# Where the modulation's last four vectors are computed: beside the delta-net heads, or beside the branch merge

## The chip, the cores and the metric

One Trainium2 chip, one of its cores. The kernel is one program that runs once. The time is device microseconds (us) of that run. The kernel before took 2231.86 us (median of 3 runs, 2228.46 to 2231.94). The engines are named as in the profile: PE (matrix unit; PEld its weight loads), DVE (vector), ACT (scalar), POOL (general), and SP, which here only issues DMAs.

## The reference

One layer of a streaming encoder, on x of 1024 positions by 1024 channels, all in float32. The parts that matter here, shortened:

```python
mod = (silu(c) @ w_ada + b_ada)[:, None, :]            # 1024 -> 6 * 1024
shift_t, scale_t, gate_t, shift_f, scale_f, gate_f = split(mod, 6)
h = x * (1 + scale_t) + shift_t
proj = h @ w_in                                        # split into the inputs of both branches
o_a = gated_deltanet(...)                              # 8 heads, chunked delta rule
o_b = chunk_band_attention(...)                        # 16 heads, 9-chunk band
merged = gate_a * (o_a @ w_branch_a) + gate_b * (o_b @ w_branch_b)
x = layernorm(ALPHA * x + gate_t * (merged @ w_o))
h = x * (1 + scale_f) + shift_f
...                                                    # up-projection, conv, product, down-projection
x = layernorm(ALPHA * x + gate_f * ffn)
```

`shift_t` and `scale_t` are needed at once. The other four vectors of `mod` are needed late: `gate_t` when `w_o` is prepared in the merge, `shift_f` and `scale_f` after the first layer norm, `gate_f` in the down-projection. They are what is moved: 4096 numbers, each a dot product of 1024 terms.

## The kernel before, in words

Large products are made exact by splitting each float32 operand in a high part (a cast by ACT) and a low part (the rest: source minus high part, by DVE or POOL), and adding three matmuls: high by high, high by low, low by high. A weight block of 1024 x 128 is loaded by one DMA of 512 KB into a tile `raw`, cast to `wh` on ACT and subtracted to `wl` on POOL (`wblock`, L275). `raw`, `wh` and `wl` have three buffers each. They are handed out in the order in which the code asks for them: a load into `raw` can be issued only when the tile three requests earlier has been read for the last time. All these loads are on SP's queue, which issues in its own order and stops at the first one that may not start.

The stages are: modulation of x and first projections (to about 90 us); eight delta-net heads, each with a triangular solve, an inverse and a chain over 8 steps, with projections woven between them (to about 870); sixteen attention heads (to about 1347); the merge (L1036 to L1077), which starts while attention still runs; the output projection `mix` with layer norm (from 1459.5); up- and down-projection.

The merge has two branches of eight blocks. Below, a0 to a7 are the blocks of branch A and b0 to b7 those of branch B. A block is 48 matmuls, 24 for each half of the positions, into one PSUM bank (`pbr`). Branch A's banks are 0 and 1: DVE's scaling by the gate (`ma`, L1054) frees a bank. Branch A multiplies `o_a`, which lies in `hh` and `hl`. Branch B multiplies `o_b`, whose eight row blocks are loaded back from `ob_d` through `raw` and split (`load_split`, L1065): ob0 and ob1 are asked for after a5, ob2 to ob4 after a6, ob5 to ob7 after a7. During branch B the rows of `w_o` also pass through `raw`: they are scaled by `gate_t` (L1075) and split.

The four late vectors were made in `mod_rows` (L804), called twice per head. Sixteen halves m0 to m15, two for each 512 columns: a half loads four 128 x 512 pieces of `w_ada` in two DMAs through `raw`, and DVE multiplies each by `silu(c)` and adds it to an accumulator (`gt` ring, 2 slots, shared with the gates' outputs). After an odd half PE sums the accumulator over partitions with a matrix of ones (`pmod`), DVE adds the bias, and the row goes to memory (`mod_d`). After the merge `shift_f` and `scale_f` came back from `mod_d` and were transposed on PE (`pmr`, L1119).

The code is handed to a scheduler that simulates the program and fixes each engine's order in advance. Engines then run in that order and wait for each other by semaphores.

Of the kernel before, what the change touches and what calls it, by code (L numbers as in the profile page):

```python
# [17 lines left out]
P = 128  # L18
# [55 lines left out]
def _at(group, step_, n, first=0):  # L74
    return tuple((group, first + step_ * i) for i in range(n))
# [26 lines left out]
    "bt": _at("GA", 640, 2), "sb": (*_at("GA", 640, 4, 1280), ("FA", 384)),  # L102
    "ot": (("GA", 3840), ("FA", 0)), "mx": _at("FA", 4, 8, 256),

    "gb": _at("GB", 512, 2), "macc": _at("M", 0, 1), 
    "st": _at("ST", 12, 2), "mv": _at("ST", 4, 4, 36), "gtb": (MA[0],), "g1b": (_E1[1],),
    "b1b": (_E1[2],), "r": (_E1[3], ("GL", 0)), "x1": _at("GL", 1024, 2, 1024),
    "h2": _at("GL", 0, 1, 3072),
# [46 lines left out]
def hybrid_layer(  # L155
# [646 lines left out]
    macc = [None]  # L802

    def mod_rows(i):  # L804

        cb = i // 2
        if i % 2 == 0:
            macc[0] = ring("gt", [P, 512])
        acc = macc[0]
        for k0 in range(4 * (i % 2), 4 * (i % 2) + 4, 2):  # L810
            rv = W.tile([P, 2, 512], F32, tag="raw", bufs=RB, name=nm("raw"))
            SP.dma_start(rv, w_ada2[k0 * P:(k0 + 2) * P,
                                    2 * D + 512 * cb:2 * D + 512 * cb + 512].rearrange(
                                        "(k p) n -> p k n", p=P))
            for k in (k0, k0 + 1):
                if k == 0:
                    DVE.tensor_scalar(acc, rv[:, 0, :], csil[:, 0:1], None, ALU.mult)
                else:
                    DVE.scalar_tensor_tensor(acc, rv[:, k - k0, :], csil[:, k:k + 1], acc,
                                             ALU.mult, ALU.add)  # L820
        if i % 2 == 1:
            pr_ = mtile(nm("pmod"), "i")
            PE.matmul(pr_, ones, acc, start=True, stop=True)
            row = ring("gt", [P, 512])[0:1, :]
            SP.dma_start(row, b_ada[:, 2 * D + 512 * cb:2 * D + 512 * cb + 512])
            DVE.tensor_tensor(row, row, pr_[0:1, :], ALU.add)
            SP.dma_start(mod_d[:, 512 * cb:512 * cb + 512], row)
# [13 lines left out]
    for h in range(HA):  # L841
        ORD = "sigKq"
        for o in ORD:
            if o == "s":
                with tc.high_priority(offset=PF):
                    stage_solve(h, cs[h])
            elif o == "i":
                with tc.high_priority(offset=PI):
                    stage_inverse(h, cs[h])
            elif o == "K" and h + 1 < HA:  # L850
                with tc.issue_after(last.ins) if last else nullcontext():
                    cs.append(stage_k(h + 1))
            elif o == "g":
                some_gates(GA[h])
            elif o == "q" and h + 1 < HA:
                stage_q(h + 1, cs[h + 1])
        some_gates(GB[h])
        for i in (2 * h, 2 * h + 1):
            mod_rows(i)
        if h + 1 < HA:  # L860
            stage_vz(h + 1, cs[h + 1])
        with tc.high_priority(offset=PC):
            stage_chain(h, cs[h])
        with tc.high_priority(offset=PT):
            stage_out(h, cs[h])
        last = cs[h]["last"]
# [163 lines left out]
    def bcast(key, src):  # L1030
        t_ = ring(key, [P, D])
        SP.dma_start(t_, src.partition_broadcast(P).rearrange("p o n -> p (o n)"))
        return t_

    wo = []
    for br in range(2):  # L1036
        if br == 1:
            mh, ml = (t_.rearrange("p k s -> p (k s)").rearrange("p (t k q) -> p t k q", t=NT, k=NK)
                      for t_ in (hh, hl))
        rh, rl = ((oahk, oalk), (obh, obl))[br]  # L1040
        for j in range(NK):
            w = wblock(kview(wbr[br], j * P, P), NK)
            for n in range(2):
                N = slice(512 * n, 512 * n + 512)
                ps = pbank(nm("pbr"), "ab"[br])
                for k in range(NK):
                    for a, r in ((w[0], rh), (w[0], rl), (w[1], rh)):
                        PE.matmul(ps, a[:, k, :], r[k][:, N],  # L1048
                                  start=(k == 0 and a is w[0] and r is rh),
                                  stop=(k == NK - 1 and a is w[1]))  # L1050
                gt_ = ma[j][:, N] if br == 0 else ring("gb", [P, 512])
                SP.dma_start(gt_, gates_d[br * NK + j][:, N])
                if br == 0:
                    DVE.scalar_tensor_tensor(gt_, gt_, 1.0, ps, ALU.add, ALU.mult)  # L1054
                else:
                    DVE.scalar_tensor_tensor(gt_, gt_, 1.0, ps, ALU.add, ALU.mult)
                    POOL.tensor_tensor(gt_, gt_, ma[j][:, N], ALU.add)
                    T4 = slice(4 * n, 4 * n + 4)
                    split(mh[:, T4, j, :], ml[:, T4, j, :],
                          gt_.rearrange("p (t q) -> p t q", t=4), ACT, DVE)  # L1060
                    if "merged" in dbg:
                        SP.dma_start(dbg["merged"][j * P:j * P + P, N], gt_)
            if br == 0:
                for k in {5: (0, 1), 6: (2, 3, 4), 7: (5, 6, 7)}.get(j, ()):
                    load_split(obh[k], obl[k], ob_d[k], ACT, DVE)  # L1065
            if br == 1 and j == 0:
                gtb = bcast("gtb", mod_d[:, 0:D])
                DVE.tensor_scalar(gtb, gtb, 0.5, None, ALU.mult)
            if br == 1 and j and (j % 2 == 0 or j == NK - 1):

                for k in ([j // 2 - 1] if j < NK - 1 else range(3, NK)):
                    a, b = (place(o, [P, D], F32R, "wo") for o in (*MA[1:], *OB[:9])[2 * k:2 * k + 2])
                    raw = W.tile([P, D], F32, tag="raw", bufs=RB, name=nm("raw"))
                    SP.dma_start(raw, w_o2[k * P:k * P + P, :])
                    DVE.tensor_tensor(raw, raw, gtb, ALU.mult)  # L1075
                    split(a, b, raw, ACT, DVE)
                    wo.append((a, b))  # L1077
# [508 lines left out]
```

## Time and profile before

| What | us |
|---|---|
| median of 3 runs | 2231.86 |
| the profiled execution: its own time | 2233.05 |
| its span, first to last instruction | 2231.3 |
| attention's last matmul, from where PE only does merge blocks | 1346.15 |
| last merge block ends, `mix` begins | 1459.52 |

The profile is of one execution. A row of a timeline gives the start, the duration, the engine, the line, what is written from what, and in brackets how long the engine stood idle before it and who ended that. Several instructions of a kind are merged in a row with xN. Rows with SPq are DMA issues. Matmuls overlap in the pipeline, so a matmul of 392 ns is followed by the next after about 228 ns. A full-precision product is recorded as two matmuls.

### The profile page before, as it was taken

To read this page: it belongs to the slowest core of one execution; us is meant where nothing else is said; L and a number is where in the kernel's file an instruction comes from. 1 tells how busy PE (TensorE), PEld (TensorE's weight loads), DVE (VectorE), ACT (ScalarE), POOL (GpSimd) and SP (SyncE) were. 2 spreads that over 40 slices of the span, in tenths; PEclk is the share of its full clock that TensorE was granted. 3 is DMA by queue.
4 is the path that set the end of the run, shared out by engine and by line. 5 is a ranking of instruction groups with operands and counts; after the bars stand their busy time and mean duration, and the time that the engine had idled before them with its cause. 6 is when DMAs were issued, how large, how long until landed. Compare 5 with 4: busy or idle time off the path is not lost.

```text
span 2231.3 us, 31605 instructions
## 1 busy us (share of the span) xinstructions
PE 2129.5 (95%) x11469; PEld 1781.7 (80%) x11469; DVE 1575.9 (71%) x3234; ACT 1032.8 (46%) x2196; POOL 607.2 (27%) x554
## 2 busy tenths in 40 slices
PE   6998999999999999999999999999899999999997
PEld 5787787777878787798989788888688888888875
DVE  7467585765667764567776653456998888889998
ACT  4645253434434334467675642234554444455532
POOL 4323232332222322234342423433010000000064
PEclk9999999999999999999999999999999999999999
DMA  9232333423232412211111424342222222243213
GB/s 277 83 110 79 95 92 106 119 74 112 81 98 92 135 36 84 80 53 51 60 63 63 148 95 132 109 137 95 65 96 85 85 85 85 85 189 129 108 48 132
DMA packets 227263, 220.48 MB, mean 99 GB/s; under 512 B 27354, under 2 KB 184467, under 8 KB 227107
## 3 DMA queue, kind: packets, MB, share of 16 engines
q1 hardware_dynamic: 227027, 218.44, 30.9%
q8 instruction: 90, 1.47, 0.3%
q14 instruction: 66, 0.54, 0.1%
q10 hardware_dynamic: 80, 0.03, 0.0%
HBM read 177.48 MB, written 47.23 MB: 101 GB/s over the span
## 4 chain that ended last, share of the span: by engine, by line
PE 45%; DVE 6%; issue 1%; ACT 1%; DMA 0%; POOL 0%; DVEq 0%; SPq 0%; ACTq 0%
PE pup L1296 18%; PE pbr L1048 8%; PE pdn L1470 6%; PE pwo L1110 4%; PE pqk L885 2%; PE pv L900 2%; PE po L975 2%; PE pp L960 1%; PE ps L934 1%; DVE hh L1536 0%; DVE hh L1507 0%; DMA raw<-in_w_branch_a_dram 0%; DVE dop L181 0%; DVE hl L181 0%; DVE hh L1506 0%
## 5 line engine op out<-in xcount | busy, mean ns | idle before, releaser
L181 POOL TENSOR_TENSOR wl<-raw,wh 128x1024 fp32r<-128x1024 f32 x88 | 211.7, 2408 | 325.1 <-ACT wh L178 295.6
L1296 PE MATMUL pup<-hh,wop 128*128 128x512 f32 x704 | 226.8, 392 | 0.4 <-ACT hh L178 0.4
L1296 PE MATMUL pup<-t,wop 128*128 128x512 f32 x792 | 191.3, 395 | 5.5 <-DVE wop L181 3.3
L1296 PEld LDWEIGHTS pup<-t,wop 128*128 128x128 f32 x792 | 149.6, 189 | 39.5 <-DVE wop L181 3.7
L1296 PEld LDWEIGHTS pup<-hh,wop 128*128 128x128 f32 x704 | 133.0, 189 | 29.5 <-ACT hh L178 0.8
L178 ACT CAST wh<-raw 128x1024 fp32r<-128x1024 f32 x88 | 92.4, 1050 | 136.3 <-DMA raw<-in_w_in_dram 57.3
L285 PE MATMUL pqkv<-hh,wh 128*128 128x512 f32 x352 | 143.3, 408 | 0.0
L285 PE MATMUL pqkv<-hl,wh 128*128 128x512 f32 x352 | 141.2, 401 | 0.0
L285 PE MATMUL pqkv<-hh,wl 128*128 128x512 f32 x352 | 140.0, 399 | 0.0
L1296 PE MATMUL pup<-hl,wop 128*128 128x512 f32 x352 | 137.9, 392 | 1.7 <-DVE hl L181 1.7
L664 DVE TENSOR_TENSOR FT<-FT,G 128x16 f32<-128x16 f32 (+30 forms) x248 | 120.7, 487 | 19.5 <-POOL G L609 12.2
L178 ACT CAST wop<-wr 128x512 fp32r<-128x512 f32 x110 | 67.8, 621 | 124.7 <-DVE wr L1282 62.9
L945 POOL TENSOR_SCALAR G<-G,FT 128x640 f32<-128x640 f32 (+4 forms) x103 | 69.9, 681 | 182.9 <-DVE FT L944 161.9
L1337 POOL TENSOR_TENSOR cc<-cc,G 128x512 f32<-128x512 f32 x15 | 26.2, 1751 | 265.7 <-DVE G L1319 222.7
L181 DVE TENSOR_TENSOR wop<-wr,wop 128x512 fp32r<-128x512 f32 x110 | 80.7, 740 | 25.1 <-ACT wop L178 25.0
L285 PE MATMUL pgt<-hh,wl 128*128 128x512 f32 x240 | 95.1, 396 | 0.8 <-POOL wl L181 0.8
L285 PE MATMUL pgt<-hh,wh 128*128 128x512 f32 x240 | 95.4, 397 | 0.1
L285 PE MATMUL pgt<-hl,wh 128*128 128x512 f32 x240 | 94.7, 395 | 0.0
L964 DVE TENSOR_TENSOR pl<-pp,ph 128x512 fp32r<-128x512 f32 (+2 forms) x116 | 72.5, 635 | 17.2 <-ACT ph L963 16.4
L1470 PE MATMUL pdn<-hl 128*128 128x512 f32 x324 | 78.2, 395 | 4.9 <-DVE hh L1484 4.6
L942 ACT ACTIVATE G<-G,FT 128x640 f32<-128x640 f32 (+4 forms) x103 | 71.6, 696 | 18.9 <-DVE FT L937 16.9
L1296 PEld LDWEIGHTS pup<-hl,wop 128*128 128x128 f32 x352 | 66.6, 189 | 16.2 <-DVE hl L181 2.1
(457 smaller groups left out, 6163.2 us busy)
## 6 DMA issues: line engine op xcount, KB each, us to landing
raw<-in_w_in_dram SPq DMA_DIRECT2D x72, 512.0 KB
wr<-in_w_up_dram SPq DMA_DIRECT2D x44, 512.0 KB
raw<-in_w_ada_dram SPq DMA_DIRECT2D x32, 512.0 KB
dr<-g_d SPq DMA_DIRECT2D x18, 512.0 KB
dr<-in_w_down_dram SPq DMA_DIRECT2D x18, 512.0 KB
wa<-in_w_ada_dram SPq DMA_DIRECT2D x32, 256.0 KB
gates_d<-GT SPq DMA_DIRECT2D x32, 256.0 KB
g_d<-yy SPq DMA_DIRECT2D x15, 512.0 KB
```

What stands on the lines that cost most here:

```text
L178: ACT.copy(h, src)
L181: return le.tensor_tensor(l, src, f(h), ALU.subtract).ins
L285: PE.matmul(ps, a[:, k, :], r[k][:, 512 * n:512 * n + 512], start=(k == 0 and a is wh and r is rh), stop=(k == NK - 1 and a is wl))
L664: DVE.tensor_tensor(pr[:, :, 0:i + 1], ft[:, :, 0:i + 1], fa[:, i:i + 1, 0:i + 1].to_broadcast([P, 8, i + 1]), ALU.mult)
L885: PE.matmul(ps, a[:, k, :], r[:, k, 512 * n:512 * n + 512], start=(k == 0 and a is w[0] and r is hh), stop=(k == NK - 1 and a is w[1]))
L942: ACT.activation(sb[:, 0:n], sb[:, 0:n], AF.Exp, bias=mx[:, nb - 1:nb], scale=-1.0, accum_out=mx[:, 2:3])
L945: POOL.tensor_scalar(sb[:, 0:n], sb[:, 0:n], mx[:, 3:4], 0.0, ALU.mult, ALU.add)
L964: DVE.tensor_tensor(pl[:, B, :], pp, f(ph[:, B, :]), ALU.subtract)
L1048: PE.matmul(ps, a[:, k, :], r[k][:, N], start=(k == 0 and a is w[0] and r is rh), stop=(k == NK - 1 and a is w[1]))
L1110: PE.matmul(ps[n], a[:, t, k, :], wo[k][b][:, 512 * n:512 * n + 512], start=(k == 0 and a is mh and b == 0), stop=(k == NK - 1 and a is ml))
L1296: PE.matmul(ps, a[:, u, k, :], b[v][k], start=(new and k == 0 and u == 0 and v == 0), stop=(k == 3 and u == 1), skip_group_check=not new)
L1470: PE.matmul(sets[s_][i], a[:, u, i * P:i * P + P], b[:, v, :], start=(new and j == 0 and u == 0 and v == 0), stop=(j == nq - 1 and u == 1) ...
```

## The change

The halves m0 to m15 leave the delta-net heads. They are now made by `mod_half`, which a table places behind blocks of the merge: m0 and m1 behind a5, m2 and m3 behind a6, m4 behind a7, and eleven halves behind b0 to b6. The accumulator has a ring of two slots of its own (in the space `B4`). For `gate_t` and `gate_f` the row goes to memory as before. For `shift_f` and `scale_f` four small matmuls by one column of ones put the sums straight into columns, and DVE adds the bias from `vt` there, so the load and the transpose after the merge are gone. In the merge, the block of branch weights is asked for two blocks ahead of its use in the code.

```diff
-    "gb": _at("GB", 512, 2), "macc": _at("M", 0, 1), 
+    "gb": _at("GB", 512, 2), "macc": _at("M", 512, 2), 
...
-    def mod_rows(i):
...
-        for i in (2 * h, 2 * h + 1):
-            mod_rows(i)
...
+    def mod_half(i):
+        cb = i // 2
+        if i % 2 == 0:
+            macc[0] = ring("macc", [P, 512])
+        acc = macc[0]
...
+        if i % 2 == 0:
+            return
+        pr_ = pbank(nm("pmod"), "mod")
+        if 2 <= cb < 6:
+            for q in range(4):
+                PE.matmul(pr_[:, q:q + 1], acc[:, q * P:q * P + P], ones[:, 0:1], start=True, stop=True)
+            o, v = 8 + 4 * (cb - 2), VO["b_ada"] + 16 + 4 * cb
+            DVE.tensor_tensor(aff[:, o:o + 4], pr_[:, 0:4], vt[:, v:v + 4], ALU.add)
+        else:
+            PE.matmul(pr_, ones, acc, start=True, stop=True)
+            row = acc[0:1, :]
...
+    MODS = {(0, 5): (0, 1), (0, 6): (2, 3), (0, 7): (4,), (1, 0): (5, 6), (1, 1): (7,), (1, 2): (8, 9), (1, 3): (10,),
+            (1, 4): (11, 12), (1, 5): (13,), (1, 6): (14, 15)}
+    def branch_block(i):
+        return wblock(kview(wbr[i // NK], i % NK * P, P), NK)
+    wnext = [branch_block(i) for i in range(2)]
...
-            w = wblock(kview(wbr[br], j * P, P), NK)
+            w = wnext.pop(0)
+            if NK * br + j + 2 < 2 * NK:
+                wnext.append(branch_block(NK * br + j + 2))
...
+            for i in MODS.get((br, j), ()):
+                mod_half(i)
             if br == 0:
                 for k in {5: (0, 1), 6: (2, 3, 4), 7: (5, 6, 7)}.get(j, ()):
                     load_split(obh[k], obl[k], ob_d[k], ACT, DVE)
...
-    mrow = ring("macc", [P, P])[0:16, :]
-    SP.dma_start(mrow, mod_d[:, D:3 * D].rearrange("o (r p) -> (o r) p", p=P))
-    pmr = pbank("pmr", "t")
-    PE.transpose(pmr[:, 0:16], mrow, ident[0:16, 0:16])
```

What stands where now, at three places. First SP's queue at the end of attention. Before, with `raw_12899` the weights of a7, ob0 to ob2 already ahead of it and `ob_d<-ob_12023` the store of the last attention output:

```order
L186 DMA raw_12899<-in_w_branch_a_dram 128x8x128
L186 DMA raw_12893<-ob_d 128x1024
L186 DMA raw_12961<-ob_d 128x1024
L186 DMA raw_13040<-in_w_branch_b_dram 128x8x128
L1117 DMA B_1594_12402<-mod_d 16x128
L186 DMA raw_12889<-ob_d 128x1024
L1013 DMA ob_d<-ob_12023 128x1024
L1052 DMA FT_12403<-gates_d 128x512 x2
L186 DMA raw_12965<-ob_d 128x1024
L186 DMA raw_12957<-ob_d 128x1024
```

Of the change, from the weights of a7 (`raw_12604`) on, `ob_d<-ob_11855` being the same store:

```order
L186 DMA raw_12604<-in_w_branch_a_dram 128x8x128
L1018 DMA raw_12662<-in_w_ada_dram 128x2x512
L1018 DMA raw_12666<-in_w_ada_dram 128x2x512
L1018 DMA raw_12670<-in_w_ada_dram 128x2x512
L1018 DMA raw_12674<-in_w_ada_dram 128x2x512
L984 DMA ob_d<-ob_11855 128x1024
L1068 DMA FT_12235<-gates_d 128x512 x2
L186 DMA raw_12683<-ob_d 128x1024
L186 DMA raw_12687<-ob_d 128x1024
L186 DMA raw_12693<-in_w_branch_b_dram 128x8x128
L1018 DMA raw_12751<-in_w_ada_dram 128x2x512
```

The loads of m0 and m1 stand ahead of the store now, and all eight loads of `ob_d` behind it; before, six of them stood ahead.

Second, DVE in the change, from the half of a4 that it scales second (`pbr_12575`); L1023 and L1025 are the products of m0 and m1, `ob_11855` is the last attention output that waits for PE, L181 is the split of ob0. Before, none of the L1023 and L1025 stood here:

```order
L1070 SCALAR_TENSOR_TENSOR ma_12241<-ma_12241,pbr_12575 128x512
L1023 TENSOR_SCALAR B_1554_12234<-raw_12662,csil 128x512
L1025 SCALAR_TENSOR_TENSOR B_1554_12234<-raw_12662,csil,B_1554_12234 128x512
L952 TENSOR_TENSOR ob_11855<-po_12217,FT_7141 64x256
L1025 SCALAR_TENSOR_TENSOR B_1554_12234<-raw_12666,csil,B_1554_12234 128x512 x2
L1070 SCALAR_TENSOR_TENSOR ma_12242<-ma_12242,pbr_12608 128x512
L1025 SCALAR_TENSOR_TENSOR B_1554_12234<-raw_12670,csil,B_1554_12234 128x512 x2
L1025 SCALAR_TENSOR_TENSOR B_1554_12234<-raw_12674,csil,B_1554_12234 128x512 x2
L1070 SCALAR_TENSOR_TENSOR ma_12242<-ma_12242,pbr_12635 128x512
```

The scalings that free branch A's banks stand behind products that need a load.

Third, PE in the change, where a6 ends (`pbr_12724`), a7 begins (`pbr_12790`) and the second half of a7 (`pbr_12817`) is cut by `pmod`. Before, each half's 24 matmuls stood together and in the order of the blocks. `pbr_12870` is b0:

```order
L1064 MATMUL pbr_12724<-hh,wl_12543 128x512
L1064 MATMUL pbr_12870<-ob_12245,wh_12691 128x512
L1064 MATMUL pbr_12870<-ob_12251,wh_12691 128x512
L1064 MATMUL pbr_12870<-ob_12245,wl_12692 128x512
L1064 MATMUL pbr_12870<-ob_12246,wh_12691 128x512
L1064 MATMUL pbr_12790<-hh,wh_12602 128x512
```

And a little further on:

```order
L1064 MATMUL pbr_12817<-hh,wh_12602 128x512
L1064 MATMUL pbr_12817<-hl,wh_12602 128x512
L1036 MATMUL pmod_12767<-B_1554_12234,ones 128x512
L1064 MATMUL pbr_12817<-hh,wl_12603 128x512
L1064 MATMUL pbr_12817<-hh,wh_12602 128x512
```

Four matmuls of b0 stand ahead of a7, and PE must have m3 finished to go on in a7. Further on PE's row has b0, its second half and b1 in pieces: 11 of b0's first half, 15 of its second, 4 of b1, then the rest mixed.

More of the change, by code (lines that the diff above doesn't have):

```diff
@@ L800, in gate_block @@
             SP.dma_start(gates_d[j][:, N], gt_)
-    macc = [None]
-    def mod_rows(i):
[L806 to L827, printed above, removed]
     gate_block(0)
@@ L1033, in bcast @@
         return t_
+    aff = cst.tile([P, 24], F32, tag="aff", name="aff")
+    macc = [None]
+    def mod_half(i):
[3 more added lines that the diff above has]
+        acc = macc[0]
+        for k0 in range(4 * (i % 2), 4 * (i % 2) + 4, 2):
+            rv = W.tile([P, 2, 512], F32, tag="raw", bufs=RB, name=nm("raw"))
+            SP.dma_start(rv, w_ada2[k0 * P:(k0 + 2) * P,
+                                    2 * D + 512 * cb:2 * D + 512 * cb + 512].rearrange(
+                                        "(k p) n -> p k n", p=P))
+            for k in (k0, k0 + 1):
+                if k == 0:
+                    DVE.tensor_scalar(acc, rv[:, 0, :], csil[:, 0:1], None, ALU.mult)
+                else:
+                    DVE.scalar_tensor_tensor(acc, rv[:, k - k0, :], csil[:, k:k + 1], acc,
+                                             ALU.mult, ALU.add)
+        if i % 2 == 0:
[6 more added lines that the diff above has]
+            DVE.tensor_tensor(aff[:, o:o + 4], pr_[:, 0:4], vt[:, v:v + 4], ALU.add)
+        else:
+            PE.matmul(pr_, ones, acc, start=True, stop=True)
+            row = acc[0:1, :]
+            SP.dma_start(row, b_ada[:, 2 * D + 512 * cb:2 * D + 512 * cb + 512])
+            DVE.tensor_tensor(row, row, pr_[0:1, :], ALU.add)
+            SP.dma_start(mod_d[:, 512 * cb:512 * cb + 512], row)
+    MODS = {(0, 5): (0, 1), (0, 6): (2, 3), (0, 7): (4,), (1, 0): (5, 6), (1, 1): (7,), (1, 2): (8, 9), (1, 3): (10,),
[3 more added lines that the diff above has]
+    wnext = [branch_block(i) for i in range(2)]
     wo = []
@@ L1115, in hybrid_layer @@
     ps, nxt = mix(0), mix(1)
-    mrow = ring("macc", [P, P])[0:16, :]
-    SP.dma_start(mrow, mod_d[:, D:3 * D].rearrange("o (r p) -> (o r) p", p=P))
-    pmr = pbank("pmr", "t")
-    PE.transpose(pmr[:, 0:16], mrow, ident[0:16, 0:16])
-    aff = cst.tile([P, 24], F32, tag="aff", name="aff")
-    g1f, b1f, s1 = aff[:, 0:8], aff[:, 8:16], aff[:, 16:24]
+    b1f, s1, g1f = aff[:, 8:16], aff[:, 16:24], aff[:, 0:8]
     g1c, b1c = vt[:, VO["ln1g"]:VO["ln1g"] + 8], vt[:, VO["ln1b"]:VO["ln1b"] + 8]
-    DVE.tensor_scalar(s1, pmr[:, 8:16], 1.0, None, ALU.add)
+    DVE.tensor_scalar(s1, s1, 1.0, None, ALU.add)
+    DVE.tensor_tensor(g1f, s1, b1c, ALU.mult)
+    DVE.tensor_tensor(b1f, b1f, g1f, ALU.add)
     DVE.tensor_tensor(g1f, s1, g1c, ALU.mult)
-    DVE.tensor_tensor(b1f, s1, b1c, ALU.mult)
-    DVE.tensor_tensor(b1f, pmr[:, 0:8], b1f, ALU.add)
     late, t2f = [], []
```

## The prediction

> **What bounds the kernel now.** I read the page's busy times first, then its chain.
>
> ```profile
> PE 2129.5 (95%) x11469; PEld 1781.7 (80%) x11469; DVE 1575.9 (71%) x3234; ACT 1032.8 (46%) x2196; POOL 607.2 (27%) x554
> PE pup L1296 18%; PE pbr L1048 8%; PE pdn L1470 6%; PE pwo L1110 4%; PE pqk L885 2%; PE pv L900 2%; PE po L975 2%; PE pp L960 1%; PE ps L934 1%; DVE hh L1536 0%; DVE hh L1507 0%; DMA raw<-in_w_branch_a_dram 0%; DVE dop L181 0%; DVE hl L181 0%; DVE hh L1506 0%
> ```
>
> PE is busy 95% of the span and the chain runs through it; the merge (`pbr`) and `mix` (`pwo`) stand in it. So work that leaves DVE is worth what PE waits for it. Next, by stretches: two of the heads, then the part of the merge after attention, then `mix`'s start. Columns: stretch, its length, busy PE, PEld, DVE, ACT, POOL, clock share, DMA share, GB/s.
>
> ```profile
> 90.00:450.00 360.00, 346.40 (x2049) 284.73 (x2047) 244.01 (x612) 155.97 (x402) 106.55 (x108) 0.99 0.35 102
> 450.00:800.00 350.00, 333.78 (x1958) 275.02 (x1955) 238.41 (x583) 136.29 (x394) 104.06 (x92) 0.99 0.33 96
> 1346.00:1460.00 114.00, 114.00 (x503) 94.11 (x503) 51.12 (x52) 27.06 (x33) 39.27 (x23) 1.00 0.39 125
> 1460.00:1480.00 20.00, 20.00 (x88) 16.10 (x88) 12.32 (x19) 5.86 (x8) 1.82 (x1) 1.00 0.63 213
> ```
>
> In the heads PE idles 13.6 + 16.2 = 29.8 us of 710. In the merge it idles nothing at all in 114 us, while DVE has 63 us and the DMAs 61% to spare. The change takes work out of a place where PE waits a little and puts it where PE does not wait. The waits of the heads, both rows of the same two stretches:
>
> ```profile
> PE pxt L688 <- DMA G<-ft_d: 5.4, 5, 1.7
> PE pvn L730 <- DVE vs L727: 2.2, 4, 0.9
> PE pks L726 <- DVE SA L741: 4.3, 2, 4.1
> PE pxt L688 <- DMA G<-ft_d: 2.5, 4, 0.9
> ```
>
> Those that DVE can shorten (its own, and the solve's result `ft_d`, which DVE computes) are 14.4 us here.
>
> **The change, part by part. What leaves the heads.**
>
> ```profile
> L817 DVE TENSOR_SCALAR GT<-raw,csil x8: 469/486/489, 160.0 to 757.5; 128x512 f32<-128x512 f32 x8
> L819 DVE SCALAR_TENSOR_TENSOR GT<-raw,csil,GT x56: 706/752/2939, 160.7 to 770.3; 128x512 f32<-128x512 f32 x56
> L826 DVE TENSOR_TENSOR GT<-GT,pmod x8: 665/676/676, 227.3 to 862.9; 1x512 f32<-1x512 f32 x8
> DVE GT L817 <- DMA gates_d<-GT: 15.6, 5, 4.0
> 224.29 0.39 PE L285 MATMUL pgt<-hh,wh 128*128 128x512 f32 x1
> 224.51 1.02 PE L823 MATMUL pmod<-GT,ones 128*128 128x512 f32 x2
> 224.97 0.79 PE L285 MATMUL pgt<-hl,wh 128*128 128x512 f32 x1
> 225.60 0.39 PE L285 MATMUL pgt<-hh,wl 128*128 128x512 f32 x1
> ```
>
> On PE: from the start of `pmod` at 224.51 to that of the second product behind it at 225.60 are 1.09 us, of which one ordinary step (224.29 to 224.51, 0.22) is the product's own. So a `pmod` costs 0.87, and eight cost **6.9 us**, all on PE's row. On DVE: 8 x 0.486 + 56 x 0.752 + 8 x 0.676 = 51.4 us, and 15.6 us in which DVE stood behind a gate's store because the accumulator took a slot of the gates' ring. DVE is not the bound, so this is worth only what it shortens of the 14.4 us. Between 0 and 14.4 I take **5**: a seventh of DVE's time goes (67 of 482 busy), but the solve's chain keeps its own latency and PE's order is made anew, which moves its waits rather than ends them. It could as well add 5.
>
> **What the branch weights gain.** Asking for them two blocks ahead gains nothing that the rows show:
>
> ```profile
> 1337.68 1.05 ACT L178 CAST wh<-raw 128x1024 fp32r<-128x1024 f32 x1 [3.58 <-PE pbr L1048]
> 1371.91 1.05 ACT L178 CAST wh<-raw 128x1024 fp32r<-128x1024 f32 x1 [3.73 <-PE pbr L1048]
> 1338.81 2.40 POOL L181 TENSOR_TENSOR wl<-raw,wh 128x1024 fp32r<-128x1024 f32 x1 [12.22 <-ACT wh L178]
> ```
>
> The cast already waits for PE to end a block and free one of three `wh`: it is two blocks ahead now. I cost it at nothing. Its order in the `raw` ring matters, though: a7's weights hold a `raw` until 1338.81 + 2.40 = 1341.2.
>
> **What the merge gets on PE.** Four wide `pmod`, 4 x 0.87 = 3.5. Sixteen small products, 32 recorded matmuls; bounds 0 and 32 x 0.250 = 8.0 by the row below, which is a duration and not a step; I take 2.2, under a third, since a step is shorter than its duration (0.22 against 0.39 above) and one column moves instead of 512. Minus the transpose `pmr`, under 0.3.
>
> ```profile
> L398 PE MATMUL pmods<-ones,G x32: 164/250/372, 10.1 to 59.0; 128*128 128x1 f32 x32
> ```
>
> **What the merge gets in waits.** Here I walk through the `raw` ring, on the clock of before. The durations:
>
> ```profile
> 1348.35 0.33 SPq L186 DMA_DIRECT2D raw<-ob_d  x1
> 1353.03 1.05 ACT L178 CAST ob<-raw 128x1024 fp32r<-128x1024 f32 x1 [5.58 <-DMA raw<-ob_d]
> 1249.73 0.38 SPq L186 DMA_DIRECT2D raw<-in_w_branch_a_dram  x1
> 1256.38 1.04 ACT L178 CAST wh<-raw 128x1024 fp32r<-128x1024 f32 x1 [2.26 <-DMA raw<-in_w_branch_a_dram]
> 1361.73 1.23 DVE L181 TENSOR_TENSOR ob<-raw,ob 128x1024 fp32r<-128x1024 f32 x1 [1.45 <-ACT ob L178]
> 1348.36 0.43 DVE L981 TENSOR_TENSOR ob<-po,FT 64x256 f32<-64x256 f32 x1
> 1348.81 0.35 SPq L1013 DMA_DIRECT2D ob_d<-ob  x1
> ```
>
> A load in long rows lands after 4.7 us, one of branch weights after 6.6. A `raw` is then held 1.5 us by a load of a half (two products), 2.3 by an ob (cast 1.05, subtract 1.23), 3.5 by weights (1.05 + 2.40). In before the last ob was split at 1363.0, and b0 began at about 1371.7: 8.7 us to spare.
>
> Now. m0's first load is used after a4's scaling, m0's second only behind the last attention output (1348.36 + 0.43), since DVE's row has it so. That puts a5's first scaling at 1351, not 1343.6, and a6, due at 1350.2, waits 1.5 for its bank. m1 ends at 1354. SP issues ob0 behind the store and two gate loads, at 1351, ob1 at 1352.5, b0's weights at 1354. With three buffers it goes on: ob0 and ob1 split by 1359.5, b0's weights by 1364.2, m2 done at 1366.8, m3 at 1372.7, ob2 to ob4 split at 1373.9, 1377.5, 1379.7, b1's weights at 1384.0, m4 at 1386.6, ob6 at 1390.6, ob5 at 1391.8, ob7 at 1393.7: 30 us later than before.
>
> PE over it: a6 ends at 1363.5 with its `pmod`; four matmuls of b0 wait for `wl` until 1364.7; a7 waits for its bank until 1365.4; its second half waits for m3 until 1372.7 and ends at 1378.6; b0 and its second half take what is there until 1384.6, then four of b1 until 1385.5. Then PE has nothing until ob5 is cast at 1390.4. The 62 matmuls left of b0 and b1 take 14.1 us at 0.2277, and b1 ends at 1405.5 against 1371.7 + 96 x 0.2277 = 1393.6. The step is 113.37 us over 498:
>
> ```profile
> 1346.15 113.37 PE pbr L1048 x498
> 1459.52 8.28 PE pwo L1110 x36
> ```
>
> So 11.9 us by the end of b1, of which 2.3 are sums already counted: **9.6 us of waits**. After a wait PE is slow for a while:
>
> ```profile
> 1257.48 0.50 PE L1048 MATMUL pbr<-hh,wh 128*128 128x512 f32 x1 [1.96 <-ACT wh L178]
> 1260.97 0.63 PE L1048 MATMUL pbr<-hl,wh 128*128 128x512 f32 x1
> 1261.39 0.63 PE L1048 MATMUL pbr<-hh,wl 128*128 128x512 f32 x1
> ```
>
> 3.5 us after an idle of 1.96 a step is 0.42 instead of 0.228. I add **1**. The Trainium skill ("TensorE: Matmul & The Clock Gate", Part 1) says that a window of about 3.4 us idle halves the array's clock until a busy one has passed. By the page's figure a wait of 4.9 us would cost up to some 2 us more, an estimate; the row agrees in the factor and shows that less idle than the page's window can do it.
>
> From b2 on, 36 loads follow ob7 in the ring. In the walk 18 loads took 1341.2 to 1393.7, 2.9 us each; 36 more end at 1498. `mix` would begin at 1459.5 + 16.4 = 1476 and reach the last row of `w_o` 19 us later (96 matmuls, 12 of them on the last row), at 1495; with its split it is some 4 us late. By the least hold (4.7 + 1.5, a third of it: 2.1 each) it is early. I take **2**. DVE has 15 halves of 3.0 us more here, 45 us in its 63 spare.
>
> **Sum**, against the profiled execution's own 2233.05 (1.2 above the median): heads -6.9 - 5; merge +3.5 + 2.2 - 0.2 + 9.6 + 1 + 2 = +18.1. 2233.05 + 6.2 = **2239**.
>
> **Rivals.** *The ring keeps up* (faster). The DMA share is 0.39 in the merge and 0.63 at 213 GB/s; 30 loads of 0.52 MB in 134 us add 118 GB/s to 125. If loads land in 3.8 us, as one of `w_o` did alone, and the bank waits are short, the merge costs only its products, 5.5, and the heads may give 10 of the 14.4: 2233 + 5.5 - 17 = 2222 to 2227.
>
> ```profile
> 1410.47 0.33 SPq L1074 DMA_DIRECT2D raw<-in_w_o_dram  x1
> 1414.30 1.23 DVE L1075 TENSOR_TENSOR raw<-raw,gtb 128x1024 f32<-128x1024 f32 x1 [2.65 <-DMA raw<-in_w_o_dram]
> ```
>
> *Both cancel*: waits of 5 instead of 12.6, or heads that give as much as the merge costs: 2233. *DVE or the ring bounds all of branch B* (slower). The mechanism: each DVE operation behind a POOL one waits for its end. It decides once DVE's row is full.
>
> ```profile
> 1406.96 2.40 POOL L181 TENSOR_TENSOR wl<-raw,wh 128x1024 fp32r<-128x1024 f32 x1
> 1407.04 3.40 DVE L181 TENSOR_TENSOR wo<-raw,wo 128x1024 fp32r<-128x1024 f32 x1 [1.46 <-POOL FT L1057]
> ```
>
> The subtraction of 1.23 took 3.40 beside POOL's 2.40. With 23 POOL operations in the stretch, each holding one new product by about half of its mean 1.7 us, DVE has 51 + 45 + 20 = 116 us in 130; adding the waits for loads in its order it may fall 14 us further behind than my sum: 2253. The Trainium skill ("SBUF — State Buffer", section "SBUF: two separate sides") calls this an exclusive lock that an operation holds to its end, for DVE operations with two SBUF inputs against POOL. The new products have two; by that rule this rival would be the likelier the more POOL works, and the row agrees. *The change does not do what it says*, in that the weights come no earlier, is part of my sum.
>
> **How the numbers follow.** Forecast 2239 (2235 to 2247): 0.40. Ring keeps up: 0.25. Cancel: 0.21. Branch B bound: 0.14. Faster or slower by 0.2%, 4.5 us, is about what a measurement of this kernel can tell from no change; against the median 2231.86 slower begins at 2236.3. The forecast's lower end is inside the bound, a little of it counts there. Faster 0.25, same 0.23, slower 0.52. The range takes in both rivals' middles and the heads' bounds: 2223 to 2256.
>
> **What would show it.** Right: PE waits in the merge of some 10 us in sum, named for DVE's `ma`, the accumulator and ob5, the last ob split near 30 us after attention's end more than before, and PE's idle of 29.8 us in the heads down by about 5. Wrong: no PE idle between attention and `mix`, then the loads land faster than 4.7 us; or waits in b2 to b7, then DVE's row is the bound; or the heads' idle moves by more than 10 us either way, which my 5 cannot carry.

## The result, and the profile after

| | us, median | against before, with 95% interval |
|---|---|---|
| before | 2231.05 (4 runs, 2228.46 to 2231.94) | |
| after | 2245.68 (4 runs, 2245.43 to 2248.19) | 1.0076 (1.0061 to 1.0090) |

The change makes the kernel slower by 0.6 to 0.9%. The profiled execution of after took 2248.19 us, with a span of 2246.5. First the page's busy times and its chain, by engine and by line:

```profile
PE 2132.5 (95%) x11492; PEld 1781.9 (79%) x11492; DVE 1581.2 (70%) x3234; ACT 1036.2 (46%) x2198; POOL 607.7 (27%) x554
PE 39%; DVE 8%; DMA 4%; issue 2%; ACT 1%; POOL 0%; SPq 0%; DVEq 0%; ACTq 0%; POOLq 0%
PE pup L1309 18%; PE pdn L1483 6%; PE pwo L1128 4%; PE pbr L1064 3%; PE pqk L856 2%; DMA raw<-in_w_ada_dram 2%; PE pv L871 2%; PE po L946 2%; PE pp L931 1%; PE ps L905 1%; DVE B L1025 1%; DMA raw<-ob_d 1%; DVE hl L181 1%; DVE hh L1549 0%; DVE hh L1520 0%
```

The shares of the engines hardly move. The chain does: the branch matmuls `pbr` fall from 8% to 3%, and in their place stand the loads of `w_ada` (2%), the products made of them (`B`, L1025) and the loads of `ob_d`. So in the merge PE is no longer what sets the end. The windows show it (columns as in the prediction). The first two are the fixed stretches of the heads, the third runs from the last attention matmul to the first of `mix`, the fourth is the start of `mix`:

```profile
90.00:450.00 360.00, 345.44 (x2057) 283.92 (x2056) 222.94 (x576) 156.85 (x403) 104.94 (x107) 0.99 0.26 77
450.00:800.00 350.00, 344.64 (x2112) 291.69 (x2110) 225.99 (x606) 143.59 (x418) 102.82 (x96) 1.00 0.25 73
1319.90:1469.20 149.30, 133.07 (x556) 106.84 (x555) 105.36 (x127) 29.56 (x35) 40.94 (x22) 0.93 0.66 217
1469.20:1570.70 101.50, 97.39 (x442) 79.52 (x440) 59.16 (x86) 40.99 (x75) 38.43 (x21) 0.97 0.34 116
```

In the heads PE idles 14.6 + 5.4 = 20.0 us of the 710, where it was 29.8. In the merge it idles 16.2 us where it idled nothing, its granted clock is 0.93 where it was 1.00, and the DMA share is 0.66 where it was 0.39.

Milestones in the two traces tell how much went each way. A milestone is the start of a tile's first or last matmul:

| milestone | before | after | difference |
|---|---|---|---|
| first attention score (`ps`), where the heads end | 864.3 | 842.0 | -22.3 |
| last attention output (`po`) | 1345.9 | 1319.9 | -26.0 |
| first matmul of `mix` (`pwo`) | 1459.4 | 1469.2 | +9.8 |
| first matmul of the up-projection (`pup`) | 1554.0 | 1570.7 | +16.7 |

Some 4 of the 26.0 are no gain: 18 more branch matmuls now stand behind the last attention output (516 where 498 stood), at 0.228 us each. The heads give 22; from the last attention output on, the merge takes 36 more, these 4 among them, and `mix` 7. What PE waits for in the merge and in `mix` (us in total, times, longest), and the waits where they are:

```profile
PE pmod L1032 <- DVE B L1025: 10.5, 3, 6.5
PE pmod L1036 <- DVE B L1025: 2.5, 1, 2.5
PE pbr L1064 <- ACT ob L178: 2.5, 1, 2.5
PE pwo L1128 <- ACT wo L178: 2.1, 1, 2.1
PE pwo L1128 <- DVE wo L181: 2.0, 1, 2.0
PE pmod L1036 <- DVE B L1039: 0.7, 1, 0.7
```

```profile
1361.37 1.03 PE L1064 MATMUL pbr<-ob,wh 128*128 128x512 f32 x3 [2.51 <-ACT ob L178]
1372.29 1.02 PE L1032 MATMUL pmod<-ones,B 128*128 128x1 f32 x8 [1.54 <-DVE B L1025]
1393.61 1.84 PE L1032 MATMUL pmod<-ones,B 128*128 128x1 f32 x8 [6.49 <-DVE B L1025]
1395.31 0.77 PE L1064 MATMUL pbr<-ob,wh 128*128 128x512 f32 x1
1395.88 0.63 PE L1064 MATMUL pbr<-ob,wl 128*128 128x512 f32 x1
1396.31 1.05 PE L1064 MATMUL pbr<-ob,wh 128*128 128x512 f32 x2
1426.68 1.54 PE L1032 MATMUL pmod<-ones,B 128*128 128x1 f32 x8 [2.44 <-DVE B L1025]
1445.68 1.10 PE L1036 MATMUL pmod<-B,ones 128*128 128x512 f32 x2 [2.54 <-DVE B L1025]
```

13.7 of the 20.3 us are waits at `pmod`. Nothing in the merge needs the sums that it waits for: shift and scale are used after `mix`'s first layer norm, `gate_f` later still. They stand in PE's row ahead of branch matmuls, and PE keeps its row. What the accumulator waits for is in DVE's row around the longest of them:

```profile
1385.96 0.75 DVE L1025 SCALAR_TENSOR_TENSOR B<-raw,csil,B 128x512 f32<-128x512 f32 x1 [0.99 <-DMA raw<-in_w_ada_dram]
1389.71 3.75 DVE L1025 SCALAR_TENSOR_TENSOR B<-raw,csil,B 128x512 f32<-128x512 f32 x2 [0.95 <-DMA raw<-in_w_ada_dram]
1397.74 0.75 DVE L1025 SCALAR_TENSOR_TENSOR B<-raw,csil,B 128x512 f32<-128x512 f32 x1 [2.48 <-DMA raw<-in_w_ada_dram]
```

Both suspects are here: products that wait for their load, and a pair that takes 3.75 us in the place of 1.5. The trace alone doesn't say which of them sets the time. The experiments do.

### The profile page after: what moved, and what is told of

Its sections match the earlier page's. It is cut to its first block, busy times and chain, and to the rows that moved or that the text cites. A ratio compares the mean times of both kernels' runs of the same rounds, so it can differ in the third digit from the quotient of the medians.

```text
span 2246.5 us, 31681 instructions
## 1 busy us (share of the span) xinstructions
PE 2132.5 (95%) x11492; PEld 1781.9 (79%) x11492; DVE 1581.2 (70%) x3234; ACT 1036.2 (46%) x2198; POOL 607.7 (27%) x554
## 4 chain that ended last, share of the span: by engine, by line
PE 39%; DVE 8%; DMA 4%; issue 2%; ACT 1%; POOL 0%; SPq 0%; DVEq 0%; ACTq 0%; POOLq 0%
PE pup L1309 18%; PE pdn L1483 6%; PE pwo L1128 4%; PE pbr L1064 3%; PE pqk L856 2%; DMA raw<-in_w_ada_dram 2%; PE pv L871 2%; PE po L946 2%; PE pp L931 1%; PE ps L905 1%; DVE B L1025 1%; DMA raw<-ob_d 1%; DVE hl L181 1%; DVE hh L1549 0%; DVE hh L1520 0%
## 5 line engine op out<-in xcount | busy, mean ns | idle before, releaser
L181 POOL TENSOR_TENSOR wl<-raw,wh 128x1024 fp32r<-128x1024 f32 x88 | 212.3, 2415 | 336.0 <-ACT wh L178 317.9
L664 DVE TENSOR_TENSOR FT<-FT,G 128x16 f32<-128x16 f32 (+30 forms) x248 | 121.1, 488 | 12.1 <-POOL G L609 4.8
L181 DVE TENSOR_TENSOR wop<-wr,wop 128x512 fp32r<-128x512 f32 x110 | 80.9, 741 | 20.9 <-ACT wop L178 20.6
L913 ACT ACTIVATE G<-G,FT 128x640 f32<-128x640 f32 (+4 forms) x103 | 71.5, 695 | 20.9 <-DVE FT L908 19.2
L1309 PEld LDWEIGHTS pup<-hl,wop 128*128 128x128 f32 x352 | 66.8, 190 | 16.2 <-DVE hl L181 2.1
```

Of the source, the lines that this page charges most:

```text
L181: return le.tensor_tensor(l, src, f(h), ALU.subtract).ins
L664: DVE.tensor_tensor(pr[:, :, 0:i + 1], ft[:, :, 0:i + 1], fa[:, i:i + 1, 0:i + 1].to_broadcast([P, 8, i + 1]), ALU.mult)
L913: ACT.activation(sb[:, 0:n], sb[:, 0:n], AF.Exp, bias=mx[:, nb - 1:nb], scale=-1.0, accum_out=mx[:, 2:3])
L1309: PE.matmul(ps, a[:, u, k, :], b[v][k], start=(new and k == 0 and u == 0 and v == 0), stop=(k == 3 and u == 1), skip_group_check=not new)
```

## The experiments

In each, the ratio is against runs of the kernel before on the same chip, whose medians lay between 2229.6 and 2230.5.

### Which stage pays, and what the weights two blocks ahead do

The halves left out of the changed kernel altogether:

```diff
-            for i in MODS.get((br, j), ()):
-                mod_half(i)
```

> Leaves the last four vectors out altogether: neither their loads, nor their products, nor their sums (the scale, shift and gates that use them are ones). Theory: everything that the changed kernel loses, it loses by these halves in the merge, and what it gains, it gains by their absence from the heads. The gain in the heads is the distance by which the last attention output came earlier (1345.9 to 1319.9, 26 us) less about 4 us of branch matmuls that stood ahead of it, so 22 us: 2207 to 2213 us, and the merge from the last attention output to the first w_o matmul within 3 us of the 111 us it took before. Rival (the weights two blocks ahead cost something of their own in the merge, by the order of the raw buffers): 2215 us or more, with PE waits for ACT or DVE of obh, wh or wl in the merge. If the heads gained only the 12 us that the prediction gave them: 2219 to 2222.

Measured: 2210.03 us, 0.9905 (0.9890 to 0.9921). The first window runs from the last attention output to the first matmul of `mix`, the second is the start of `mix`:

```profile
1318.90:1435.60 116.70, 116.70 (x517) 96.30 (x516) 53.47 (x54) 29.05 (x35) 39.70 (x23) 1.00 0.40 129
1435.60:1531.30 95.70, 94.51 (x440) 77.62 (x439) 54.97 (x83) 39.16 (x73) 35.30 (x20) 1.00 0.35 118
```

PE is busy throughout at the full clock, and the heads end where they do in after (first score at 842.1). So the heads' gain is 20 us by the medians, and everything that the changed kernel loses is the halves' doing in the merge and in `mix`: 2245.7 - 2210.0 = 35.7. In the two profiles the merge is 149.3 - 116.7 = 32.6 longer and `mix` 5.8. The merge was 116.7, not within 3 of the 111 that I had named. From the last attention output to `mix` before took 113.5 by the milestones, not 111, and some 4 us of matmuls of branch A moved behind that output.

The kernel before with only the weights asked for ahead, and the changed kernel with each block's weights asked for at their own block:

```diff
-            w = wblock(kview(wbr[br], j * P, P), NK)
+            w = wnext.pop(0)
+            if NK * br + j + 2 < 2 * NK:
+                wnext.append(branch_block(NK * br + j + 2))
```

> The kernel before, with the branch weights asked for two blocks ahead and nothing else. Theory (costed at nothing): 2227 to 2235 us, no difference that can be measured. Rival: the weights take raw buffers ahead of the second branch's inputs, and PE waits for these: 2236 us or more.

Measured: 2229.87 us, 0.9998 (0.9985 to 1.0010): nothing.

> The changed kernel with each branch block's weights asked for at its own block again. Theory (the products' loads hold the ring, whatever the order of the weights): 2241 to 2255 us, no faster than the changed kernel's 2246, and PE then waits for the branch weights (wl by DVE or POOL) as well as for the accumulator. Rival (the weights ahead delay the second branch's inputs and the halves): 2240 us or less.

Measured: 2267.22 us, 1.0159 (1.0142 to 1.0177), by the ratios 0.8% or some 20 us above the changed kernel. The direction was expected, the size wasn't. PE's waits in the merge of this kernel:

```profile
PE pbr L1061 <- ACT wh L178: 10.8, 3, 4.4
PE pmod L1036 <- DVE B L1025: 9.8, 2, 8.6
PE pmod L1032 <- DVE B L1025: 3.7, 2, 2.1
```

Asking ahead is worth nothing in the kernel before, and some 20 us where the halves' loads stand in the same ring: without it the cast of the next block's weights (`wh`) is late by 10.8 us in sum, which is not in after's list at all.

### Loads or DVE's time

First the sums alone, then the products without loads, then the loads nearly without products. In the first two the operand is a tile that is already in the chip's memory:

```diff
-            rv = W.tile([P, 2, 512], F32, tag="raw", bufs=RB, name=nm("raw"))
-            SP.dma_start(rv, w_ada2[k0 * P:(k0 + 2) * P,
...
+            if k0 == 0:
+                DVE.tensor_scalar(acc, ma[0][:, 0:512], csil[:, 0:1], None, ALU.mult)
```

> The changed kernel with the eight sums on PE, each of one product of a tile that is already there: 32 loads and 56 products are left out. Every theory: 2210 plus PE's own 5.7 us, 2213 to 2218 us; more than that would say that the sums' banks or their place in PE's row cost time without any late operand.

Measured: 2220.13 us, 0.9963 (0.9951 to 0.9974).

```diff
-            rv = W.tile([P, 2, 512], F32, tag="raw", bufs=RB, name=nm("raw"))
-            SP.dma_start(rv, w_ada2[k0 * P:(k0 + 2) * P,
...
+            rv = ma[0].rearrange("p (k n) -> p k n", k=2)
```

> The changed kernel with all 64 products and all eight sums at their places, but the products read a tile that is already in the chip's memory (a product of branch A): the 32 loads of w_ada in the merge, and their turns of the raw buffers, are left out. Theory (the products wait for their loads through the raw ring, which 40 MB in some 150 us keep full): what is left is PE's own work on the sums, 4 x 0.87 + 32 x 0.07 = 5.7 us, and DVE's share beside POOL: 2214 to 2222 us. Rival (DVE is the bound in branch B, its products stretched beside POOL): 2230 to 2246 us, with DVE busy above nine tenths and waits at pmod.

Measured: 2223.48 us, 0.9975 (0.9964 to 0.9985), just above the theory's figure. The 40 MB that it names were too many: 217 GB/s over the 149.3 us of after's merge are 32.

```diff
-                    DVE.tensor_scalar(acc, rv[:, 0, :], csil[:, 0:1], None, ALU.mult)
+                    DVE.tensor_scalar(acc, ones[:, 0:1].to_broadcast([P, 512]), csil[:, 0:1], None, ALU.mult)
...
-                    DVE.scalar_tensor_tensor(acc, rv[:, k - k0, :], csil[:, k:k + 1], acc,
+                DVE.scalar_tensor_tensor(acc[:, 0:8], rv[:, k - k0, 0:8], csil[:, k:k + 1], acc[:, 0:8],
```

> The changed kernel with all 32 loads of w_ada and eight sums, but each product made over 8 of the 512 columns: DVE's work on them nearly left out (64 products of some 0.7 us become 0.1). Theory (the loads' turns of the raw ring are what the sums wait for): 2232 to 2246 us, with PE's waits at pmod still 8 us or more. Rival (DVE's time): 2214 to 2222 us.

Measured: 2243.16 us, 1.0066 (1.0045 to 1.0088). The merge of the three, in this order, each from its last attention output to its first matmul of `mix`:

```profile
1316.70:1440.50 123.80, 123.80 (x557) 101.37 (x555) 63.00 (x72) 28.55 (x34) 39.62 (x23) 1.00 0.36 119
```

```profile
1316.40:1441.80 125.40, 124.06 (x557) 101.31 (x555) 102.95 (x125) 27.19 (x33) 42.73 (x22) 1.00 0.34 112
```

```profile
1319.80:1465.30 145.50, 130.25 (x557) 104.39 (x555) 75.20 (x137) 29.92 (x36) 37.05 (x22) 0.95 0.68 224
```

This is the clearest reading of the study. With all products and no loads DVE is busy 103 of 125 us, nearly as many as the 105 in after, and PE idles 1.3 us. With all loads and DVE at 75 of 146, PE idles 15.3 us, nearly the 16.2 of after. So the loads cost 2245.7 - 2223.5 = 22.2 us, DVE's time on the products only 2245.7 - 2243.2 = 2.5, which is within the noise of the two runs. Added to the sums alone in place of taken from the whole, they come out the same: 2243.2 - 2220.1 = 23.1 for the loads and 2223.5 - 2220.1 = 3.4 for the products.

The DMA engines aren't full at a share of 0.68. What holds the loads back is seen in what SP's queue waits for in the merge of after:

```profile
SPq L1018 <- DVE B L1025: 21.0, 13, 3.8
SPq L186 <- DVE B L1025: 16.4, 10, 3.7
SPq L1068 <- DVE hl L181: 16.2, 13, 5.3
```

L1018 are the halves' loads, L186 those of the weights and of `ob_d`. Together they stand 37.4 us until a product has read a buffer of the ring for the last time. So the ring of three does hold loads back. It isn't alone: the gates' loads (L1068) stand in the same queue for 16.2 us until a slot of their own is free, and the loads behind them stand too. How the 22 us divide between ring and queue is open. A fourth buffer wasn't tried.

The sums alone cost 10.1 us by the medians, 2220.1 - 2210.0, more than I had reckoned (5.7). In the profiles it is 123.8 - 116.7 = 7.1 us in the merge, all of it PE's busy time, and 2.3 in `mix`. A group of four small sums and the steps behind it, in after:

```profile
1406.79 0.95 PE L1032 MATMUL pmod<-ones,B 128*128 128x1 f32 x8
1407.60 0.71 PE L1064 MATMUL pbr<-ob,wh 128*128 128x512 f32 x2
1408.14 0.40 PE L1064 MATMUL pbr<-ob,wl 128*128 128x512 f32 x1
```

From 1406.79 to 1408.14 are 1.35 us, of which two steps of 0.228 are the products' own. So the group costs 0.89, measured as the 0.87 of a sum over 512 columns was: four matmuls of one column are no cheaper than one of 512. 4 x 0.87 + 4 x 0.89 = 7.0, the 7.1 of the merge.

### The sums out of PE's way

```diff
         if i % 2 == 0:
+            if len(owed) == 2:
+                mod_sum(*owed.pop(0))
             macc[0] = ring("macc", [P, 512])
...
-        pr_ = pbank(nm("pmod"), "mod")
+        if i % 2:
+            owed.append((cb, acc))
+    def mod_sum(cb, acc):
+        pr_ = pbank(nm("pmod"), "mod")
```

> The changed kernel with the same loads and products, but each accumulator's sum (pmod) handed to PE about one block later, just before its buffer is needed again. Theory: PE stands still because pmod stands in its row ahead of branch matmuls that could run; its waits at pmod (13.7 us in the merge) and most of the slow stretches behind them go: 2218 to 2230 us. Rival (DVE and the raw ring are the bound in branch B, and each branch block is late whatever PE's order): 2238 to 2248 us, with the waits at pmod turned into waits of branch or w_o matmuls for DVE, ACT or a load.

Measured: 2236.70 us, 1.0034 (1.0023 to 1.0045). That is 9.0 us better than after and just between the two forecasts. Its merge, and its waits there and in `mix`:

```profile
1319.60:1452.40 132.80, 124.97 (x555) 100.25 (x552) 89.44 (x118) 27.77 (x33) 39.44 (x22) 1.00 0.70 226
```

```profile
PE pbr L1068 <- DVE FT L1076: 4.2, 3, 1.7
PE pwo L1134 <- ACT wo L178: 3.9, 2, 3.3
PE pmod L1036 <- DVE B L1027: 1.4, 1, 1.4
```

The waits at `pmod` fall from 13.7 to 2.3 (0.9 of it in `mix`), and the clock is back at 1.00. PE's busy time falls from 133.1 to 125.0, about that of the sums alone. The theory holds as far as it went, and its figure was missed. It had not reckoned with what is late next: PE now waits for the scaling that frees a bank of branch B (`FT`, L1076) and for the split of `w_o`. DVE's row still stops for loads ahead of such work, for 1.24 us at 1380.07 with a scaling behind it. Putting the sums later moves PE's wait, and only part of it goes.

Half of the work back in the heads (both gates there in heads 0, 2, 4 and 6; shift and scale beside the merge, one half a block, sums a block late):

```diff
+        if h % 2 == 0:
+            cb = (0, 1, 6, 7)[h // 2]
+            for i in (2 * cb, 2 * cb + 1):
+                mod_rows(i)
...
+    MODS = {(0, 6): (4,), (0, 7): (5,), (1, 0): (6,), (1, 1): (7,), (1, 2): (8,), (1, 3): (9,),
+            (1, 4): (10,), (1, 5): (11,)}
```

> Two of the four vectors (both gates, the wide sums) back in heads 0, 2, 4 and 6, the other two (shift and scale) beside the merge, one half a block from the seventh block on, with the sum a block late as in the run with late sums. Theory (the merge has room for about half of these loads: without them its DMA engines are 0.23 to 0.54 busy, with all of them 0.54 to 0.77): heads keep half of their 20 us, the merge costs PE's own 32 x 0.07 = 2.2 us and few waits: 2220 to 2228 us, faster than before. Rival (the loads cost the merge as much each, however few they are): half of the late-sum run's 26.7 us and half of the heads' 20: 2210 + 13 + 10 = 2233 us.

Measured: 2236.48 us, 1.0034 (1.0020 to 1.0048). The theory's figure is missed; the rival's 2233 is nearer. The merge itself came near the theory:

```profile
1336.90:1460.40 123.50, 120.84 (x541) 98.42 (x539) 71.78 (x84) 28.73 (x34) 38.80 (x22) 1.00 0.58 185
1460.40:1562.70 102.30, 98.93 (x450) 80.98 (x450) 61.32 (x93) 40.78 (x76) 36.10 (x21) 0.97 0.37 121
```

It took 6.8 us more than without halves, where 2.2 and few waits were expected, and idled 2.7. But `mix` took 6.6 more, with a wait of 3.4 us there for a late sum, and the heads ended at 854.5, having kept about half of their gain.

### What the heads pay for

The heads gave 20 us where I had forecast 12. Four runs of the kernel before, each with one part of the halves in the heads changed. The sums as matmuls of one column:

```diff
-            PE.matmul(pr_, ones, acc, start=True, stop=True)
+            for q in range(4):
+                PE.matmul(pr_[:, q:q + 1], acc[:, q * P:q * P + P], ones[:, 0:1], start=True, stop=True)
```

> The kernel before, all halves in the heads, but each of the eight sums made as four matmuls of one column (as the changed kernel makes shift and scale) in the place of one of 512 columns. Theory A (half or more of the heads' 20 us is PE's own time for eight wide sums: eight of them and sixteen small ones took 10 us alone in the merge): 8 x (0.87 - 0.28) = 4.7 us at least go, 2221 to 2226 us, faster than before and than the changed kernel. Theory B (the heads' 20 us is DVE's products standing in its row ahead of the chain's steps, whatever the sums): 2226 to 2231 us.

Measured: 2243.80 us, 1.0071 (1.0058 to 1.0084). Neither theory has it slower. The saving of 4.7 it started from isn't there, as the 0.89 us above show (and the merge that it refers to has four wide sums, not eight). Why it is 14 us slower I can't say. The run changes more than the sums: the results leave as columns, and the gates' are stored in single numbers, in 10.1 us from issue to landing by the median. That this costs the heads something is a rival that no run here tests.

The sums alone, and everything but the sums:

```diff
-        for k0 in range(4 * (i % 2), 4 * (i % 2) + 4, 2):
...
+        if i % 2 == 0:
+            DVE.tensor_scalar(acc, ones[:, 0:1].to_broadcast([P, 512]), csil[:, 0:1], None, ALU.mult)
```

> The kernel before with its eight wide sums in the heads, each of one product of a tile of ones: 32 loads and 56 products are left out. Theory A (the sums' own time on PE is most of the heads' 20 us): 2218 to 2224 us, that is 8 to 14 us above the 2210 of the run without halves. Theory B (loads and DVE's products are most of it): 2212 to 2217 us.

Measured: 2230.96 us, 1.0007 (0.9997 to 1.0017), more than either theory has.

```diff
-            PE.matmul(pr_, ones, acc, start=True, stop=True)
...
-            DVE.tensor_tensor(row, row, pr_[0:1, :], ALU.add)
+            DVE.tensor_tensor(row, row, acc[0:1, :], ALU.add)
```

> The kernel before with all 32 loads and 64 products in the heads, but without the eight sums on PE (each row takes the accumulator's first partition in place of the sum over all). Theory A (the sums are what the heads pay for, since sums alone cost them 20 us): 2207 to 2216 us, as without any halves. Theory B (any of the two parts, sums or loads with products, brings the heads into another order that costs about as much): 2222 to 2232 us.

Measured: 2227.47 us, 0.9982 (0.9973 to 0.9992), as theory B has it. So the sums alone cost the heads 20.9 us, the loads and products alone 17.4, and both together 20. The parts do not add up: taking away either one gives next to nothing, taking away both gives all. What both have in common is the accumulator's slot in the `gt` ring, and the row that is made of it in the same ring, with its load, its addition and its store. Of the run with sums alone, then of the one without, DVE's waits in the heads:

```profile
DVE GT L811 <- DMA gates_d<-GT: 9.6, 3, 4.3
DVE GT L811 <- DMA qk_d<-GT: 3.7, 1, 3.7
```

```profile
DVE GT L817 <- DMA gates_d<-GT: 11.6, 5, 4.0
DVE GT L817 <- DMA qk_d<-GT: 2.7, 1, 2.7
```

DVE's first write to an accumulator stands up to 4.3 us until a gate's result has left the slot, and what DVE does for the delta-net heads next stands behind it in its row. After has no such wait. The last run took it away by gathering the products in the loaded buffers:

```diff
-                    DVE.scalar_tensor_tensor(acc, rv[:, k - k0, :], csil[:, k:k + 1], acc,
+                    DVE.scalar_tensor_tensor(v, v, csil[:, k:k + 1], macc[0], ALU.mult, ALU.add)
+                macc[0] = v
```

> The kernel before, all halves and sums in the heads, but the products gather in the loaded buffers themselves (each reads the buffer of the one ahead of it) in the place of an accumulator in gt, the ring of two slots that the gates' results leave through. In the kernel before, and in the three runs with something of the halves in the heads, DVE's first product stands 13 to 20 us in all waiting for a gate's store to leave its slot, with the chain's steps behind it in DVE's row; in the changed kernel there is no such wait. Theory C (this wait is the common part that the sums alone and the products alone pay for): the wait goes, the heads get back most of their 20 us but the sums' own 7: 2213 to 2224 us, faster than both kernels. Theory B (whatever stands in the heads brings them into an order that costs about as much): 2225 to 2240 us with that wait gone.

Measured: 2265.45 us, 1.0167 (1.0151 to 1.0182). Both figures were missed. Of the wait for a gate's store 4.5 us are left, and a longer one of the same kind came: each buffer is now held until the next product has read it, which needs the next load. DVE's waits in the heads:

```profile
DVE raw L819 <- DMA raw<-in_w_ada_dram: 16.9, 6, 5.5
DVE raw L817 <- DMA raw<-in_w_ada_dram: 8.3, 5, 2.8
```

That run doesn't decide between the theories. Beside each other, with the end of the heads (first attention score) against 842.1 without halves. The second column is how long DVE stands ahead of the halves' work until a store or a load is done, the third how long it stands for the solve's result (`ft_d`), in us:

| kernel | DVE stands ahead of the halves' work | DVE stands for `ft_d` | heads end later by |
|---|---|---|---|
| after | none of these | 37.6 | 0 |
| half of the halves | 4.0 + 2.6 + 1.3 = 7.9 | 24.9 | 12.4 |
| sums only | 9.6 + 3.7 = 13.3 | 33.5 | 21.6 |
| before, weights asked for ahead | 15.7 + 4.0 + 2.4 = 22.1 | 13.2 | 15.7 |
| before | 15.6 + 4.0 + 3.6 = 23.2 | 12.9 | 22.2 |
| no sums | 11.6 + 7.5 + 2.7 + 2.6 + 1.8 = 26.2 | 14.7 | 18.9 |
| small sums | 13.6 + 8.4 + 3.3 + 2.5 = 27.8 | 23.2 | 27.6 |
| gathered in the loaded buffers | 16.9 + 8.3 + 4.5 + 2.8 = 32.5 | 36.7 | 49.6 |

The second and the last column go together loosely, and single profiles differ by several us: the kernel before with weights ahead, whose program for the heads is the same in kind, ended them 6.5 earlier. The third column speaks against adding the second up as a price. In before DVE stands 23.2 + 12.9 = 36.1 us, in after 37.6: where the halves make it stand, it mostly stands less for the solve. What the heads' 20 us go to stays open. Shown are the size, and that either part alone costs nearly all of it.

No version with all halves that was run beats the kernel before.

## Why the prediction was right, and where its terms were not

The sign and the range held: 2239 forecast, 2245.7 measured, in 2223 to 2256. The sum did not: two terms were too small and pulled against each other, the heads' gain by 8 to 10 and the loss in the merge and `mix` by 20. That the total came within 7 us is in part luck.

- **What leaves the heads** was put at 6.9 + 5 = 11.9; it was 20 by the run without halves, 22 in the profile. The mechanism held. The 6.9 for the sums' own time fits the 0.87 us that a wide sum also took in the merge. The mis-sized step is the 5: PE's idle in the two stretches fell by 29.8 - 20.0 = 9.8, within its bounds of 0 to 14.4 and hardly under the 10 that the prediction had named as a sign of being wrong. (The 67 us that the prediction takes from DVE's 482 busy ones hold 15.6 of standing; 51.4 were busy.) The rest is in PE's busy time up to the first score. A cost of separate parts was the wrong model: each part alone costs nearly the whole. The window from 100 us to the first score, before:

```profile
100.00:864.30 764.30, 731.78 (x4416) 606.43 (x4415) 507.14 (x1269) 304.05 (x846) 220.69 (x220) 0.98 0.32 95
```

And after:

```profile
100.00:842.00 742.00, 719.10 (x4394) 598.91 (x4393) 456.25 (x1197) 307.35 (x850) 217.25 (x220) 0.99 0.25 74
```

PE is busy 12.7 us less. Of these 6.9 are the sums; the other 5.8, with six records fewer and a clock of 0.99 in the place of 0.98, the term did not have at all. PE idles 32.5 - 22.9 = 9.6 less. Why, the runs leave open.

- **What the branch weights gain**, nothing: right for the kernel before (0.9998), with the caution on the ring's order that the prediction made. Within the change they are worth some 20 us.
- **The sums on PE in the merge**, 3.5 + 2.2 - 0.2 = 5.5: they cost 7.1. The small ones were too cheap, 16 of them taking 4 x 0.89 = 3.6, not 2.2.
- **The walk through the ring**, 9.6 up to the end of b1: there the waits were 2.5 + 1.5 = 4.0. The late ob block came, and so did the last ob split, at 1363.8, 43.9 after the last attention output against 17.1 before: 27 more, where 30 were forecast. The walk's two other waits did not: PE ran through branch A without standing for a bank or for m3, and the 1.5 is at a later accumulator, behind b0. The walk's own last step is 1.0 too long: 1390.4 + 14.1 are 1404.5, not 1405.5.
- **The tail**, 2: this is the step that failed most. The walk stopped at b1 and costed b2 to `mix` by the one operand it had followed, the last row of `w_o`. That row was 4.1 late in sum, as the walk's own "some 4" had said. But in b2 to b7 PE waited another 6.5 + 2.4 + 2.5 + 0.7 = 12.1 at `pmod`, and the walk had not asked where the other sums stood in PE's row.
- **Slow steps after a wait**, 1: it was 133.1 - 123.8 = 9.3 in the merge, after against sums alone, whose PE has the same number of matmuls. Behind the wait of 6.49 the steps at 1395.88 are 0.43 us apart in the place of 0.228. The Trainium skill ("TensorE: Matmul & The Clock Gate", Part 1) has the array at half clock after an idle window until a busy one of about 3.4 us has passed. The trace agrees in the factor and not in the length of the idle: slow steps follow the waits of 2.51 and 2.44 as well, and none follow the one of 2.54. By the starts of the steps, the three waits that slow steps follow brought some 2, 3 and 3 us of them, an estimate. My 1, for all waits together, was too little for any of these.
- **The rival that DVE or the ring bounds branch B** (2253) was half right: the loads, in the ring and in SP's queue, not DVE's time. The prediction had said that waits in b2 to b7 would mean that DVE's row is the bound. PE does wait for DVE there, but DVE waits for loads. The Trainium skill's lock ("SBUF — State Buffer", section "SBUF: two separate sides") shows in the pair of 3.75 us, whose second product had a subtraction on POOL from 1390.13 to 1392.92 beside it. It costs little: with all products and no loads PE idled 1.3 us.

Merge and `mix` together: 18.1 forecast; 32.6 + 5.8 = 38.4 measured against the kernel without halves.

## What to carry to other kernels

Before work is moved to where an engine has time to spare, count what it needs besides time: here buffers of a ring of three and turns in a queue, which no busy share shows, and a place in the in-order row of the engine that must not wait. A sum that nobody needs yet still stops that engine if it stands ahead of work that could run. What such work costs where it stands is measured by leaving all of it out; leaving out one part at a time can show nothing each time.

## What the runs showed of the hardware that was not expected

Four full-precision matmuls with one moving column took 0.89 us of PE, one with 512 columns 0.87. And in the merge's waits, 16.2 us of idle time brought 9.3 us of slow steps behind them, but not every wait did: one of 2.44 us was followed by some 6 us of steps of 0.43, one of 2.54 by none. In the run with late sums, whose waits in the merge were at most 1.7 us long, 7.8 us of idle brought 125.0 - 123.8 = 1.2 of slow steps.
